# Last 256 columns' residual added in PSUM, last stores in three pieces, first chunk's last k tile by tile, and longer side distances in a one-core decoder trunk

## The chip, the cores and the metric

The kernel runs on one core of a Trainium2 chip. It has five engines with a queue each: TensorE (PE, matrix products and transposes), VectorE (DVE), ScalarE (ACT), GpSimd (POOL) and SyncE (SP, which here issues DMA transfers). Time is in device microseconds, the median of several executions. A profile of one execution gives the start and length of each instruction; "span" is the time from the first to the last event of the core in it.

## The reference

One layer of a decoder: RMSNorm, one input projection whose columns feed three groups (a gated short convolution, a convolution over 31 taps with layer norm, a cross-attention into 256 memory tokens), an output projection, the residual, a final RMSNorm. It is done for a prompt of 1024 tokens and for 8 samples of 8 tokens, which have states and caches of their own.

```python
h = rmsnorm(x, g_norm); proj = h @ w_in
...
out_a = bg_a * conv_a * jax.nn.silu(z_a)
out_b = jax.nn.silu(layernorm(conv_b, ln_g, ln_b)) * jax.nn.silu(z_b)
out_x = cross_attn(q, mk, mv) * jax.nn.silu(z_x)
mixed = jnp.concatenate([out_a, out_b, out_x], axis=-1)
return x + mixed @ w_out, new_ctx_a, new_ctx_b
...
y_prompt = rmsnorm(yp, g_final)
y_sample = rmsnorm(ys, g_final)
```

All is float32 (widths: model 1024, groups 384, 384 and 256).

## The kernel before

**Products in three passes.** PE multiplies values in the type `float32r`. To keep float32's precision, each operand is split into a high part (a cast, mostly on ACT) and a low part (the difference, on DVE), and a product is the sum of three: high by high, low by high, high by low. The normalized and transposed tokens are `hh` and `hl` (one pair of tiles for each k, a block of 128 of the 1024 model columns), the weights are `wh` and `wl`, the output weights `woh` and `wol`, the mixed activations `mh` and `ml`. `pass_k(n, c, ps, p, k)` is one such product: column tile n, chunk c of the tokens, pass p (0 is `hh` by `wh`, 1 is `hh` by `wl`, 2 is `hl` by `wh`), block k.

**Startup (`startup`, an order written out by hand).** The first four column tiles run over four chunks of tokens: 256, 256, 256 and 320 (`HEAD`). For the first chunk the four accumulators `acc` take up all four banks of the pool `mmp` (`MM()`); `p(k, j)` is pass j of block k for the four tiles. `x_tr` transposes a block of the raw tokens into a bank of a second pool of four (`sdp`, `SD()`), `x_ev_hi` makes `hh` of it on ACT, `x_ev_lo` makes `hl` on DVE; the bank is free after both. `n0` to `n3` are the norms of the chunks; `square` sums squares on ACT (tile `junk`, 128x1024), `r_bc` makes the factors and `r_tr` transposes them into a row `rrow`, by which DVE multiplies each accumulator of the first two chunks when it evacuates it (`evac`; the four evacuations write `u`, `u`, `u` and `sig`). The second chunk's accumulators take the same four banks, so each waits for one evacuation of the first. Weights of the first tiles are loaded in halves of 512 columns (`hw_load`), cast by `hw_hi` and subtracted by `hw_lo`.

**Side work.** After startup the order on each engine is made by a scheduler from the program's order. The projection of a tile (`proj`) calls `side()` after each four products; it takes one entry of the queue `steps`, work of another kind that PE does in between. `None` entries are distances: places at which nothing is done, so that the other engines have time for what the next entry needs. `S0` to `S3` are the distances in the sample attention: `sa_scores`, S0, `sa_norm` (DVE makes the probabilities `Ps`), S1, `sa_pT` (PE transposes `Ps`, DVE copies them to `Pts`), S2, `sa_pv` (PE multiplies `Pts` with the cached values, ACT copies to `Os`), S3, `sa_out`. Between, DVE runs the 31 taps of the second convolution (`accB`).

**Output.** `out_tile` computes a tile of 128 tokens by 1024 columns in two banks, adds the residual `xres` on DVE, sums squares on ACT, and scales and stores. The last tile is `out_last`: it goes in three parts of 512, 256 and 256 columns, and for each part DVE adds the residual out of PSUM (`xr`), ACT sums squares, and DVE multiplies with -0.5 and the final gain into `yg`. Behind the third part come root, reciprocal and one correction step (`y`, `v`, `y0`, `t`, `r`), and the scaling by r in two pieces, 576 columns on DVE and 448 on ACT, each stored by one transfer (SP and ACT issue them).

Of the kernel before, what the change touches and what calls it, by code (L numbers as in the profile page):

```python
# [10 lines left out]
F32R = mybir.dt.float32r  # L11
# [5 lines left out]
KT = 8  # L17
# [8 lines left out]
A0, A1, A2, A3, A4, A5 = 2, 9, 5, 3, 3, 1  # L26
S0, S1, S2, S3 = 4, 3, 4, 2
L0, L1, L2 = 1, 3, 2
# [13 lines left out]
def hybrid_trunk_kernel(  # L42
# [91 lines left out]
    warm = cst.tile([128, 1], F32, name="warm")  # L134
    ident = cst.tile([128, 128], F32, name="ident")
    graw = cst.tile([8, 128], F32, name="graw")
    gT = cst.tile([128, 16], F32, name="gT")
# [145 lines left out]
    def hw_hi(k, copy):  # L283
        if k % 2 == 0:
            hwh[k // 2] = B("wh", F32R, D)
            hwl[k // 2] = B("wl", F32R, D)
        copy(hwh[k // 2][:, hsl(k)], hrw[k // 2][:, hsl(k)])  # L287

# [638 lines left out]
    def out_tile(i, hook=None):  # L927
# [4 lines left out]
        for n, k in enumerate(worder):  # L932
            if hook:
                hook(n)
            for f in range(2):
                cs = slice(f * 512, f * 512 + 512)
                if sample:
                    st = ms[0][:, k * 128:k * 128 + 128]
                    mm(banks[f], st, wo_h[k][:, cs], n == 0, False, 216)
                    mm(banks[f], st, wo_l[k][:, cs], False, n == KT - 1, 216)  # L940
                else:
                    out_mm(banks[f], i, n, k, cs)
        ss = SM("oss", 2)
# [17 lines left out]

    def out_mm(bank, i, n, k, cs):
        w = cs.stop - cs.start
        a, b = mh[k][:, i * 128:i * 128 + 128], ml[k][:, i * 128:i * 128 + 128]
        mm(bank[:, :w], a, wo_h[k][:, cs], n == 0, False, w / 2.4)
        mm(bank[:, :w], b, wo_h[k][:, cs], False, False, w / 2.4)
        mm(bank[:, :w], a, wo_l[k][:, cs], False, n == KT - 1, w / 2.4)

    def out_last(i):
# [3 lines left out]
        pre = SM("opre", 1)  # L973
        parts = [slice(0, 512), slice(512, 768), slice(768, 1024)]
        for f, cs in enumerate(parts):
            w = cs.stop - cs.start
            bank = MM()
            for n, k in enumerate(worder):
                out_mm(bank, i, n, k, cs)
            V.tensor_tensor(xr[:, cs], bank[:, :w], xr[:, cs], ALU.add)  # L980
            junk = SD()
            S.activation(junk[:, :w], xr[:, cs], AF.Square, accum_out=ss[:, f:f + 1])
            if f == 1:
                V.tensor_tensor(pre, ss[:, 0:1], ss[:, 1:2], ALU.add)
                V.tensor_scalar(pre, pre, 1.0 / D, EPS, ALU.mult, ALU.add)
            V.scalar_tensor_tensor(yg[:, cs], xr[:, cs], -0.5, gf[0][:, cs], ALU.mult, ALU.mult)

# [5 lines left out]
        V.scalar_tensor_tensor(r, t, -3.0, y0, ALU.add, ALU.mult)  # L993
        a, b = slice(0, 576), slice(576, 1024)
        dst = y_prompt[0, i * 128:i * 128 + 128]
        V.tensor_scalar(yg[:, a], yg[:, a], r, None, ALU.mult)
        S.activation(yg[:, b], yg[:, b], AF.Copy, scale=r)  # L997
        nc.sync.dma_start(dst[:, a], yg[:, a])
        nc.scalar.dma_start(dst[:, b], yg[:, b])

# [6 lines left out]
    def startup():  # L1007
# [142 lines left out]
        S.copy(rrow[0][:, RAW:RAW + 256], rps[:, :256])  # L1150
        n1.square(0)
        t1 += [x_tr(1, 2), x_tr(1, 3)]
        p(7, 0)
        x_ev(1, 2, t1[2])
        x_ev(1, 3, t1[3])
        n1.square(1)
        for n in range(NHEAD):
            for j in (2, 1):
                pass_k(n, 0, acc[n], j, KT - 1, 1)
            evac(n, 0, acc[n])  # L1160
        acc = [MM() for _ in range(NHEAD)]
        for k in range(KT):
# [4 lines left out]
            if k + 4 < KT:  # L1167
                t1.append(x_tr(1, k + 4))
            if k == 3:
                r_bc(n1, 256)  # L1170
        n2.square(0)
# [184 lines left out]
```

## Time and profile before

| | |
|---|---|
| three runs | 473.11, 472.13, 474.51 us; median 473.11 |
| the profiled execution | 472.01 us, span 470.2 us |
| DVE, ACT busy | 333.4 us (71%), 229.5 us (49%) |
| HBM read and written | 34.81 MB, 5.42 MB (86 GB/s over the span) |

Times of instructions are counted from the span's start. A line of the timeline has the start, the length, the engine and line, the operation with its output and inputs (buffer numbers left out), shapes, and the count of merged instructions; in square brackets stands how long the engine stood idle before it, and who ended that. `L59` is the helper through which all of VectorE's instructions go and `L95` and `L102` are those of products and transposes, so that one has to go by the names of tiles. The view of waits has, for each pair of a waiting and a waited-for group, the sum, the number and the longest.

### The profile page before, as it was taken

To read this page: it belongs to the slowest core of one execution; us is meant where nothing else is said; L and a number is where in the kernel's file an instruction comes from. 1 tells how busy PE (TensorE), PEld (TensorE's weight loads), DVE (VectorE), ACT (ScalarE), POOL (GpSimd) and SP (SyncE) were. 2 spreads that over 40 slices of the span, in tenths; PEclk is the share of its full clock that TensorE was granted. 3 is DMA by queue.
4 is the path that set the end of the run, shared out by engine and by line. 5 is a ranking of instruction groups with operands and counts; after the bars stand their busy time and mean duration, and the time that the engine had idled before them with its cause. 6 is when DMAs were issued, how large, how long until landed. Compare 5 with 4: busy or idle time off the path is not lost.

```text
span 470.2 us, 7495 instructions
## 1 busy us (share of the span) xinstructions
PE 459.7 (98%) x2931; PEld 435.1 (93%) x2931; DVE 333.4 (71%) x593; ACT 229.5 (49%) x584; POOL 4.2 (1%) x20
## 2 busy tenths in 40 slices
PE   8999999999999999999999989999999999999994
PEld 8899999999999999999999879999999888888884
DVE  4769999999878999996899965237353537333333
ACT  5785659600223648565795364595542534111112
POOL 2000000000000000000000000000000000000000
PEclk9999999999999999999999999999999999999998
DMA  8931253100460300422021102113401634311111
GB/s 295 370 93 46 71 153 91 45 1 0 128 187 16 119 1 1 135 57 80 12 79 46 43 3 62 45 46 105 164 2 45 233 147 129 118 45 46 45 67 68
DMA packets 36447, 40.44 MB, mean 86 GB/s; under 512 B 1743, under 2 KB 30453, under 8 KB 36405
## 3 DMA queue, kind: packets, MB, share of 16 engines
q1 hardware_dynamic: 35965, 39.21, 25.7%
q10 hardware_dynamic: 448, 0.76, 0.5%
q8 instruction: 23, 0.38, 0.3%
q14 instruction: 11, 0.09, 0.1%
HBM read 34.81 MB, written 5.42 MB: 86 GB/s over the span
## 4 chain that ended last, share of the span: by engine, by line
PE 86%; DVE 11%; DMA 1%; issue 1%; ACT 1%; ACTq 0%; DVEq 0%
PE mm L95 76%; DVE accB L59 6%; PE sd L95 5%; PE sd L102 4%; DVE tA L59 1%; DVE wl L59 1%; DMA wr<-in_w_in_dram 1%; DVE red L59 1%; PE sd L874 1%; DVE mx L59 0%; DVE s L59 0%; ACT junk L187 0%; DVE hl L59 0%; ACT yg L997 0%; ACTq L1011 0%
## 5 line engine op out<-in xcount | busy, mean ns | idle before, releaser
L95 PE MATMUL mm<-hh,wh 128*128 128x384 f32 (+2 forms) x632 | 118.9, 324 | 1.1 <-DVE u L59 0.8
L95 PE MATMUL mm<-hl,wh 128*128 128x384 f32 (+2 forms) x632 | 118.6, 323 | 0.0
L59 DVE SCALAR_TENSOR_TENSOR accB<-u,prm,accB 128x1024 f32<-128x1024 f32 x90 | 115.4, 1282 | 1.5
L95 PE MATMUL mm<-hh,wl 128*128 128x384 f32 (+2 forms) x632 | 116.4, 321 | 0.0
L95 PEld LDWEIGHTS mm<-hh,wh 128*128 128x128 f32 x632 | 101.9, 188 | 2.8 <-DVE u L59 1.0
L95 PEld LDWEIGHTS mm<-hl,wh 128*128 128x128 f32 x632 | 101.7, 188 | 0.7 <-issue 0.6
L95 PEld LDWEIGHTS mm<-hh,wl 128*128 128x128 f32 x632 | 101.6, 188 | 0.4
L95 PE MATMUL mm<-woh,ml 128*128 128x512 f32 (+1 forms) x136 | 51.2, 377 | 0.0
L95 PE MATMUL mm<-wol,mh 128*128 128x512 f32 (+1 forms) x136 | 51.2, 377 | 0.0
L95 PE MATMUL mm<-woh,mh 128*128 128x512 f32 (+1 forms) x136 | 51.2, 377 | 0.0
L59 DVE TENSOR_TENSOR xres<-mm,xres 128x512 f32<-128x512 f32 (+2 forms) x19 | 12.4, 662 | 39.7 <-PE mm L95 39.5
L952 ACT ACTIVATE sd<-xres 128x512 f32<-128x512 f32 (+1 forms) x16 | 9.6, 600 | 57.9 <-DVE xres L59 57.9
L59 DVE TENSOR_TENSOR wl<-wr,wh 128x512 fp32r<-128x512 f32 x50 | 33.4, 688 | 4.2 <-ACT wh L287 2.2
L95 PEld LDWEIGHTS mm<-woh,mh 128*128 128x128 f32 x136 | 25.6, 188 | 4.7
L95 PEld LDWEIGHTS mm<-woh,ml 128*128 128x128 f32 x136 | 25.6, 188 | 4.7
L95 PEld LDWEIGHTS mm<-wol,mh 128*128 128x128 f32 x136 | 25.6, 188 | 4.6
L310 ACT CAST wh<-wr 128x512 fp32r<-128x512 f32 x42 | 24.4, 620 | 1.7 <-issue 1.3
L362 ACT ACTIVATE prod<-us,prm 128x64 f32<-128x64 f32 x93 | 24.9, 345 | 0.1
L510 ACT ACTIVATE sz<-mm 128x384 f32<-128x384 f32 (+1 forms) x24 | 11.4, 474 | 23.3 <-PE mm L95 23.1
L712 ACT ACTIVATE P<-sd,nb 128x256 f32<-128x256 f32 x32 | 14.7, 473 | 13.2 <-DVE nb L59 12.3
L433 ACT ACTIVATE sig<-mm 128x384 f32<-128x384 f32 (+1 forms) x6 | 2.8, 474 | 37.4 <-PE mm L95 37.3
L249 ACT ACTIVATE hh<-sd,gT 128x256 fp32r<-128x256 f32 (+1 forms) x32 | 14.3, 491 | 7.1 <-PE sd L102 6.8
(198 smaller groups left out, 527.9 us busy)
## 6 DMA issues: line engine op xcount, KB each, us to landing
wr<-in_w_in_dram SPq DMA_DIRECT2D x21, 512.0 KB
wor<-in_w_out_dram SPq DMA_DIRECT2D x8, 512.0 KB
xres<-in_x_prompt_dram SPq DMA_DIRECT2D x8, 512.0 KB
out_dram<-xres SPq DMA_DIRECT2D x7, 512.0 KB
x<-in_x_prompt_dram SPq DMA_DIRECT2D x6, 512.0 KB
cache<-in_cache_mem_k_dram SPq DMA_DIRECT2D x8, 256.0 KB
cache<-in_cache_mem_v_dram SPq DMA_DIRECT2D x8, 256.0 KB
wr<-in_w_in_dram SPq DMA_DIRECT2D x6, 256.0 KB
```

The costliest lines, as they stand in the source:

```text
L59: r = f(*a, **k)
L95: T.matmul(out, lhsT, rhs, start=start, stop=stop)
L102: T.transpose(out, in_, ident[:n, :n])
L249: S.activation(hh[k][:, off:off + n], ps[:, :n], AF.Copy, scale=gT[:, k:k + 1])
L310: S.copy(dst_hi[:, a:b], src[:, a:b])
L362: S.activation(p3[:, k, :], src, AF.Copy, scale=w[:, k0 + k:k0 + k + 1])
L433: S.activation(sig[j][:, off:off + n], ps[:, :n], AF.Sigmoid)
L510: S.activation(sz[0][:, off:off + n], ps[:, :n], AF.Silu)
L712: S.activation(P_[i][:, h * 256:h * 256 + 256], bank[h // 2][:, (h % 2) * 256:(h % 2) * 256 + 256], AF.Exp, bias=nb[:, h:h + 1], scale=SCA ...
L874: T.transpose(ps[:, j * 128:j * 128 + 128], accB[j][:, lncols[i]:lncols[i] + 128], ident)
L952: S.activation(junk[:rows], xr[:rows, cs], AF.Square, accum_out=ss[:rows, f:f + 1])
```

## The change

It has four parts.

1. `S1` goes from 3 to 7 and `S2` from 4 to 6: `sa_pT` stands four places later behind `sa_norm`, and `sa_pv` six places later than before.
2. In startup the last block (k = 7) of the first chunk is no longer multiplied pass by pass over the four tiles, but tile by tile with all three passes, each tile's evacuation right behind. The transposes of the next chunk's block 3 stand behind the first tile; the low parts `hl` of the blocks 2 and 3 of the next chunk stand behind the four evacuations. The squares of the second norm and its factors move later.
3. The first weight cast (`hw_hi(0)`) goes in two instructions of 256 columns instead of one of 512.
4. In `out_last` the residual of the last 256 columns is split into `rh` and `rl`, and PE adds both to the bank with a product by a unit matrix (`identr`, the cast of `ident`). DVE's addition falls away, and the square and the multiplication read the bank. The last scaling goes in three pieces: 320 and 320 columns on DVE, 384 on ACT, each with its own store.

```diff
-S0, S1, S2, S3 = 4, 3, 4, 2
+S0, S1, S2, S3 = 4, 7, 6, 2
...
-        copy(hwh[k // 2][:, hsl(k)], hrw[k // 2][:, hsl(k)])
+        c0 = (k % 2) * 512
+        for a in (range(c0, c0 + 512, 256) if k == 0 else ()):
+            copy(hwh[0][:, a:a + 256], hrw[0][:, a:a + 256])
+        if k:
+            copy(hwh[k // 2][:, hsl(k)], hrw[k // 2][:, hsl(k)])
...
+        rh, rl = B("rh", F32R, 256), B("rl", F32R, 256)
+        S.copy(identr, ident)
+        split(rh, rl, xr[:, parts[2]], 0, 256)
         for f, cs in enumerate(parts):
             w = cs.stop - cs.start
             bank = MM()
+            if f == 2:
+                mm(bank[:, :w], identr, rh, True, False, w / 2.4)
+                mm(bank[:, :w], identr, rl, False, False, w / 2.4)
             for n, k in enumerate(worder):
-                out_mm(bank, i, n, k, cs)
-            V.tensor_tensor(xr[:, cs], bank[:, :w], xr[:, cs], ALU.add)
+                out_mm(bank, i, n + (f == 2), k, cs, n == KT - 1)
+            res = bank[:, :w] if f == 2 else xr[:, cs]
+            if f < 2:
+                V.tensor_tensor(res, bank[:, :w], res, ALU.add)
             junk = SD()
-            S.activation(junk[:, :w], xr[:, cs], AF.Square, accum_out=ss[:, f:f + 1])
+            S.activation(junk[:, :w], res, AF.Square, accum_out=ss[:, f:f + 1])
...
-            V.scalar_tensor_tensor(yg[:, cs], xr[:, cs], -0.5, gf[0][:, cs], ALU.mult, ALU.mult)
+            V.scalar_tensor_tensor(yg[:, cs], res, -0.5, gf[0][:, cs], ALU.mult, ALU.mult)
...
-        a, b = slice(0, 576), slice(576, 1024)
-        V.tensor_scalar(yg[:, a], yg[:, a], r, None, ALU.mult)
-        S.activation(yg[:, b], yg[:, b], AF.Copy, scale=r)
-        nc.sync.dma_start(dst[:, a], yg[:, a])
-        nc.scalar.dma_start(dst[:, b], yg[:, b])
+        for cs in (slice(0, 320), slice(320, 640)):
+            V.tensor_scalar(yg[:, cs], yg[:, cs], r, None, ALU.mult)
+            nc.sync.dma_start(dst[:, cs], yg[:, cs])
+        cs = slice(640, 1024)
+        S.activation(yg[:, cs], yg[:, cs], AF.Copy, scale=r)
+        nc.scalar.dma_start(dst[:, cs], yg[:, cs])
...
-        n1.square(0)
-        t1 += [x_tr(1, 2), x_tr(1, 3)]
-        p(7, 0)
-        x_ev(1, 2, t1[2])
-        x_ev(1, 3, t1[3])
-        n1.square(1)
+        t1.append(x_tr(1, 2))
+        x_ev_hi(1, 2, t1[2])
         for n in range(NHEAD):
-            for j in (2, 1):
+            for j in (0, 2, 1):
                 pass_k(n, 0, acc[n], j, KT - 1, 1)
+            if n == 0:
+                t1.append(x_tr(1, 3))
+                x_ev_hi(1, 3, t1[3])
+                n1.square(0)
             evac(n, 0, acc[n])
+        x_ev_lo(1, 2, t1[2])
+        x_ev_lo(1, 3, t1[3])
...
-            if k == 3:
-                r_bc(n1, 256)
+            if k == 4:
+                n1.square(1)
+        r_bc(n1, 256)
```

**The head on DVE.** This is DVE's queue from the two oldest low parts of the second chunk (blocks 0 and 1) on, before the change. `sd` is a bank with transposed tokens, `mm` an accumulator of the first chunk.

```order
L59 SCALAR_TENSOR_TENSOR hl_125<-sd_343,gT,hh_124 128x256
L59 SCALAR_TENSOR_TENSOR hl_127<-sd_346,gT,hh_126 128x256
L59 SCALAR_TENSOR_TENSOR hl_129<-sd_371,gT,hh_128 128x256
L59 SCALAR_TENSOR_TENSOR hl_131<-sd_374,gT,hh_130 128x256
L59 TENSOR_TENSOR u_389<-mm_168,rrow_155 128x256
L59 TENSOR_TENSOR u_394<-mm_169,rrow_155 128x256
L59 TENSOR_TENSOR u_399<-mm_170,rrow_155 128x256
L59 TENSOR_TENSOR sig_404<-mm_171,rrow_155 128x256
```

And this is the same place in the change (all buffer numbers are shifted):

```order
L59 SCALAR_TENSOR_TENSOR hl_126<-sd_345,gT,hh_125 128x256
L59 SCALAR_TENSOR_TENSOR hl_128<-sd_348,gT,hh_127 128x256
L59 TENSOR_TENSOR u_384<-mm_169,rrow_156 128x256
L59 TENSOR_TENSOR u_390<-mm_170,rrow_156 128x256
L59 TENSOR_TENSOR u_396<-mm_171,rrow_156 128x256
L59 TENSOR_TENSOR sig_402<-mm_172,rrow_156 128x256
L59 SCALAR_TENSOR_TENSOR hl_130<-sd_371,gT,hh_129 128x256
L59 SCALAR_TENSOR_TENSOR hl_132<-sd_378,gT,hh_131 128x256
```

The four evacuations have moved ahead of the low parts of blocks 2 and 3.

**The head on PE.** In the change PE's queue has at that place, from the transposes of block 2 on, the following rows; `mm_169` and `mm_170` are the accumulators of tiles 0 and 1. (Before, the transposes of both blocks came first, then four `hh` by `wh` products, one for each tile, then the other passes.)

```order
L102 MATMUL sd_371<-ident,x_110 128x128
L102 MATMUL sd_371<-ident,x_115 128x128
L95 MATMUL mm_169<-hh_139,wh_311 128x256
L95 MATMUL mm_169<-hl_140,wh_311 128x256
L95 MATMUL mm_169<-hh_139,wl_312 128x256
L102 MATMUL sd_378<-ident,x_110 128x128
L102 MATMUL sd_378<-ident,x_115 128x128
L95 MATMUL mm_170<-hh_139,wh_311 128x256
L95 MATMUL mm_170<-hl_140,wh_311 128x256
L95 MATMUL mm_170<-hh_139,wl_312 128x256
```

Tile 0 is complete after three products, while the transposes of block 3 have moved behind it. On ACT the square of the second chunk's second token tile now stands between the `hh` of block 4 and of block 5; before, both squares stood ahead of block 4.

**The sample attention on PE.** Before, the transposes of `Ps` stand in the last pass of a chunk of 320 columns:

```order
L95 MATMUL mm_3120<-hl_131,wh_2860 128x320
L102 MATMUL sd_3144<-ident,Ps_3079 128x128 x2
L95 MATMUL mm_3120<-hl_133,wh_2860 128x320
L95 MATMUL mm_3120<-hl_135,wh_2860 128x320
L95 MATMUL mm_3120<-hl_137,wh_2860 128x320
L95 MATMUL mm_3120<-hl_139,wh_2860 128x320
L102 MATMUL sd_3153<-ident,Ps_3086 128x128 x2
```

In the change they stand in the second pass of the next chunk, of 384 columns:

```order
L95 MATMUL mm_3158<-hh_131,wl_3053 128x384
L102 MATMUL sd_3171<-ident,Ps_3081 128x128 x2
L95 MATMUL mm_3158<-hh_133,wl_3053 128x384
L95 MATMUL mm_3158<-hh_135,wl_3053 128x384
L95 MATMUL mm_3158<-hh_137,wl_3053 128x384
L95 MATMUL mm_3158<-hh_139,wl_3053 128x384
L102 MATMUL sd_3180<-ident,Ps_3088 128x128 x2
```

They have moved behind sixteen products. On DVE the two copies to `Pts` have moved behind the two evacuations `tA<-sz` of 384 and 320 columns and the low parts that follow these.

**The end on DVE.** The square brackets name the engines whose semaphores an instruction waits for. Before:

```order
L59 TENSOR_TENSOR xres_4579<-mm_4794,xres_4579 128x256 [waits PE_49]
L59 SCALAR_TENSOR_TENSOR yg_4731<-xres_4579,gf_3769 128x256 [waits DVE_49]
L59 SCALAR_TENSOR_TENSOR v_4824<-oss_4732,opre_4733 128x1 [waits Activation_49]
L59 RECIPROCAL y_694_4825<-y_4823 128x1 [waits Activation_49]
L59 SCALAR_TENSOR_TENSOR t_4826<-y_694_4825,v_4824 128x1 [waits DVE_49]
L59 SCALAR_TENSOR_TENSOR t_696_4827<-t_4826,y_694_4825 128x1 [waits DVE_49]
L59 TENSOR_SCALAR yg_4731<-yg_4731,t_696_4827 128x576 [waits DVE_49]
```

In the change:

```order
L59 SCALAR_TENSOR_TENSOR yg_4733<-mm_4801,gf_3771 128x256 [waits Activation_49]
L59 SCALAR_TENSOR_TENSOR v_4832<-oss_4734,opre_4735 128x1 [waits DVE_49]
L59 RECIPROCAL y_696_4833<-y_4831 128x1 [waits Activation_49]
L59 SCALAR_TENSOR_TENSOR t_4834<-y_696_4833,v_4832 128x1 [waits DVE_49]
L59 SCALAR_TENSOR_TENSOR t_698_4835<-t_4834,y_696_4833 128x1 [waits DVE_49]
L59 TENSOR_SCALAR yg_4733<-yg_4733,t_698_4835 128x320 [waits DVE_49]
L59 TENSOR_SCALAR yg_4733<-yg_4733,t_698_4835 128x320
```

The addition is gone, the multiplication reads the bank `mm` and waits for ACT (for its square of the same bank) instead of DVE, and the last scaling is two rows. On PE two products, `mm_4801<-rh_4736,identr` and `mm_4801<-rl_4737,identr`, stand ahead of the last 24.

More of the change, by code (lines that the diff above doesn't have):

```diff
@@ L135, in hybrid_trunk_kernel @@
     ident = cst.tile([128, 128], F32, name="ident")
+    identr = cst.tile([128, 128], F32R, name="identr")
     graw = cst.tile([8, 128], F32, name="graw")
@@ L941, in out_tile @@
                 else:
-                    out_mm(banks[f], i, n, k, cs)
+                    out_mm(banks[f], i, n, k, cs, n == KT - 1)
         ss = SM("oss", 2)
@@ L960, in out_tile, with out_mm @@
         nc.sync.dma_start(dst, xr[:rows])
-    def out_mm(bank, i, n, k, cs):
+    def out_mm(bank, i, n, k, cs, last):
         w = cs.stop - cs.start
@@ L966, in out_mm @@
         mm(bank[:, :w], b, wo_h[k][:, cs], False, False, w / 2.4)
-        mm(bank[:, :w], a, wo_l[k][:, cs], False, n == KT - 1, w / 2.4)
+        mm(bank[:, :w], a, wo_l[k][:, cs], False, last, w / 2.4)
     def out_last(i):
```

## The prediction

> **What bounds the kernel now.** I read the page first, then what TensorE (PE) waits for, then three places in the timeline.
>
> ```profile
> span 470.2 us, 7495 instructions
> PE 459.7 (98%) x2931; PEld 435.1 (93%) x2931; DVE 333.4 (71%) x593; ACT 229.5 (49%) x584; POOL 4.2 (1%) x20
> ...
> PE 86%; DVE 11%; DMA 1%; issue 1%; ACT 1%; ACTq 0%; DVEq 0%
> ```
>
> PE is busy for 459.7 of 470.2 us and carries 86% of the chain that ended last. So little can be won except where PE stands still, or before its first and behind its last matmul. Its waits, in the view of waits filtered to PE, leaving out the launch's own (1.4 us, not touched) and one of 0.2:
>
> ```profile
> PE sd L102 <- DVE Ps L59: 1.3, 1, 1.3
> PE mm L95 <- DVE u L59: 0.8, 1, 0.8
> PE mm L95 <- DVE wh L59: 0.3, 1, 0.3
> ```
>
> These three are what the edits of the side distances, of the head and of the start aim at. The tail is what DVE, ACT and the stores do after PE's end. I take the four places in the order of the program.
>
> **Start: the first weight cast in two halves.**
>
> ```profile
> 5.78 0.84 ACT L249 ACTIVATE hh<-sd,gT 128x256 fp32r<-128x256 f32 x2 [2.05 <-PE sd L102]
> ...
> 5.94 0.43 DVE L59 CAST wh<-wr 128x512 fp32r<-128x512 f32 x1 [0.37 <-DMA wr<-in_w_in_dram]
> ...
> 6.51 0.72 PE L95 MATMUL mm<-hh,wh 128*128 128x256 f32 x4 [0.34 <-DVE wh L59]
> ```
>
> The first product waits for the whole cast, which ends at 6.37. Half of it would be there at about 6.15; the other operand, the first of two hh at 5.78 + 0.84/2, near 6.25. The start 0.14 after the later one gives about 6.38, so **0.13 us** are won, between 0 (a later weight DMA decides) and 0.2. The second cast costs DVE a few hundredths, hidden by the 0.3 us until its next result is due. The new cast of the identity stands on ACT before the first hh, in ACT's 2.05 us of idleness there; without that cover it would cost about 0.3 (the row of 18.62 below shows 0.37 for a 128x256 ACT copy).
>
> **Head: the last k of the first chunk, tile by tile.**
>
> ```profile
> 18.62 0.37 ACT L1150 COPY rrow<-sd 128x256 f32<-128x256 f32 x1 [1.07 <-PE sd L102]
> 18.72 0.87 DVE L59 SCALAR_TENSOR_TENSOR hl<-sd,gT,hh 128x256 fp32r<-128x256 f32 x2
> 18.89 1.06 ACT L187 ACTIVATE junk<-x 128x1024 f32<-128x1024 f32 x1
> 19.05 0.44 PE L102 MATMUL sd<-ident,x 128*128 128x128 f32 x2 [0.24 <-ACT rrow L1150]
> ...
> 19.80 0.28 PE L95 MATMUL mm<-hl,wh 128*128 128x256 f32 x1
> 19.92 0.28 PE L95 MATMUL mm<-hh,wl 128*128 128x256 f32 x1
> ...
> 20.45 0.88 DVE L59 SCALAR_TENSOR_TENSOR hl<-sd,gT,hh 128x256 fp32r<-128x256 f32 x2 [0.85 <-ACT hh L249]
> ...
> 21.24 1.08 DVE L59 TENSOR_TENSOR u<-mm,rrow 128x256 f32<-128x256 f32 x3
> ...
> 21.71 1.38 PE L95 MATMUL mm<-hh,wh 128*128 128x256 f32 x4 [0.80 <-DVE u L59]
> ...
> 22.23 0.42 DVE L59 TENSOR_TENSOR sig<-mm,rrow 128x256 f32<-128x256 f32 x1
> ...
> 22.93 0.38 PE L102 MATMUL sd<-ident,x 128*128 128x128 f32 x2
> ...
> 23.34 0.47 ACT L249 ACTIVATE hh<-sd,gT 128x256 fp32r<-128x256 f32 x1 [1.21 <-PE sd L102]
> ...
> 23.62 0.38 PE L102 MATMUL sd<-ident,x 128*128 128x128 f32 x2
> ```
>
> Read it from 21.71 backwards. The second chunk's four products each need a bank that one of DVE's four evacuations (u, u, u, sig) frees. These start at 21.24 because two hl stand ahead of them in DVE's queue; the hl wait for hh, and hh for ACT's square of 1.06 us (junk). The four products then take 1.22 us instead of four times 0.12 (the step from 19.80 to 19.92).
>
> In the change the evacuations stand ahead of those two hl, and a tile's three products stand together. PE: the transposes of block 2 keep their place, tile 0's three products run from about 18.65 to 19.15, the next transposes still start at 19.05 to 19.1 (they wait for rrow, 18.62 + 0.37), and nine products at 0.12 from 19.25 issue by 20.3. DVE: the two older hl are through at 18.72 + 0.87 = 19.59; from then on one evacuation each 0.33 (from 21.24 to 22.23 are three steps), so sig starts at 20.55 instead of 22.23. The next transposes stood 0.70 behind sig (22.93); now at 21.25. That is **1.68 us** earlier.
>
> What is late next? ACT now has a square between hh of k = 4 and of k = 5. With x_tr at 21.25 and one k each 0.69 (transposes and four products, 22.93 to 23.62), PE wants k = 5 at 23.9; ACT begins hh of k = 4 at 21.66 (0.41 behind the transposes, as 23.34 behind 22.93), the square at 22.05, hh of k = 5 at 23.1 and is done by 23.6. The cover is 0.3; if it is gone, up to 0.5 is lost. Later hh follow at 0.4 on ACT against 0.48 on PE. The two hl that went behind the evacuations free their banks by 21.75, due at 22.6 and 23.3. Some rescaling moves forward on DVE between 30 and 41, the number of instructions there stays. I count 1.68 within 1.2 to 1.8.
>
> Does it last to the end? DVE is busy almost throughout from 60 to 275, so PE could run into it later. These rows speak against that:
>
> ```profile
> DVE u L59 <- ACT sig L433: 3.6, 4, 1.2
> ...
> 224.29 1.29 DVE L59 TENSOR_REDUCE mx<-sd 128x2 f32<-128x512 f32 x2 [3.02 <-PE sd L95]
> ```
>
> The first is from DVE's waits between 60 and 276, the second the place where the long DVE stretch of the chain begins: there DVE itself stood 3.02 us idle for PE. An earlier PE therefore takes DVE with it.
>
> **Sample attention: side distances S1 from 3 to 7, S2 from 4 to 6.**
>
> ```profile
> 269.76 1.55 PE L95 MATMUL mm<-hl,wh 128*128 128x384 f32 x8
> 271.14 1.33 PE L95 MATMUL mm<-hh,wh 128*128 128x320 f32 x8
> 272.31 1.34 PE L95 MATMUL mm<-hh,wl 128*128 128x320 f32 x8
> 273.48 0.75 PE L95 MATMUL mm<-hl,wh 128*128 128x320 f32 x4
> 275.57 0.41 PE L102 MATMUL sd<-ident,Ps 128*128 128x128 f32 x2 [1.34 <-DVE Ps L59]
> ```
>
> PE stands 1.34 us for Ps, with products queued behind that need nothing of it. Four more side places are 16 products, 4 of 320 and 12 of 384 columns; at 0.146 (272.31 to 273.48, eight) and 0.173 (269.76 to 271.14, eight) that is 2.66 us of work, which covers 1.34 with 1.3 to spare. So **1.34 us** go. If DVE did not follow the head's 1.8, the need would be 3.15 and 0.5 would be waited. Behind it: the two Pts copies now stand behind two evacuations on DVE, and the products that read Pts come 28 products later (4.8 us against a copy of 0.42); the output of the samples moves by six places and is still ahead of the layer norm's first transposes, whose order is unchanged. Nothing else is late.
>
> **Tail.**
>
> ```profile
> 463.58 0.28 PE L95 MATMUL mm<-wol,mh 128*128 128x256 f32 x1
> 463.90 0.42 DVE L59 TENSOR_TENSOR xres<-mm,xres 128x256 f32<-128x256 f32 x1 [1.46 <-PE mm L95]
> 464.36 0.42 DVE L59 SCALAR_TENSOR_TENSOR yg<-xres,gf 128x256 f32<-128x256 f32 x1
> 464.42 0.39 ACT L982 ACTIVATE sd<-xres 128x256 f32<-128x256 f32 x1 [2.36 <-DVE xres L59]
> ...
> 464.96 0.16 DVE L59 SCALAR_TENSOR_TENSOR v<-oss,opre 128x1 f32<-128x1 f32 x1 [0.18 <-ACT sd L982]
> ...
> 465.29 0.16 DVE L59 RECIPROCAL y<-y 128x1 f32<-128x1 f32 x1 [0.17 <-ACT y L989]
> ...
> 465.93 0.52 DVE L59 TENSOR_SCALAR yg<-yg,t 128x576 f32<-128x576 f32 x1
> ...
> 466.63 0.35 ACTq L999 DMA_DIRECT2D out_dram<-yg  x1
> ...
> 122.15 0.76 DVE L59 COPY kd<-sd 128x256 f32<-128x256 f32 x2 [0.39 <-ACT kv L664]
> ```
>
> The addition between PE's end and ACT's square goes: 464.42 - 463.90 = -0.52. Two products of 256 columns are added on PE: +0.24. The split of the residual (a cast on ACT, a subtraction on DVE) stands five output tiles earlier in the order, where both engines mostly wait for PE, and is hidden; uncovered it would be about 0.8. DVE's multiplication yg stood beside the square; now it waits for it (the order shows it) and stands ahead of v and the reciprocal. It holds DVE for 0.33 to 0.40 (the steps of u and of hl in the head), and v takes a short step more, so that the reciprocal comes, by my estimate, 0.46 behind the square's sum instead of 0.33 (464.96 to 465.29): +0.13. A wait of this kind is in the trace: at 122.15 DVE's copy of a bank waited for ACT's copy out of it, though neither reads what the other writes. The Trainium skill has the reason, in "PSUM — Partial Sum Buffer", section "PSUM bank collisions raise a hardware error": two engines must not touch one bank at once, reads included. By that rule the term is +0.13, without it 0; the trace agrees with the rule.
>
> The stores: DVE's first piece of 320 columns is ready about 0.2 sooner than 576 were, so the first transfer starts 0.2 sooner; the last issue stays near 466.65, since an issue takes 0.35 and SP has two, and ACT's piece shrinks by 64 columns of 448. I take -0.1, between -0.2 and +0.5 (three transfers of smaller rows in place of two; no row has such sizes). Tail: -0.52 + 0.24 + 0.13 - 0.1 = **-0.25**, between -0.4 and +0.35.
>
> **Sum.** 0.13 + 1.68 + 1.34 + 0.25 = 3.4 us off the span of 470.2: 466.8. The profiled execution took 472.01, 1.8 more than its span, and would become 468.6. It lies 1.1 under the median of the three runs (473.11) and at their lowest (472.13); runs scatter upwards by some 2 us, so I name 469.0 for the median.
>
> **The rivals.**
> 1. DVE takes part of the head back (0.17). If its backlog keeps its place in time, PE gains the 1.34, of the head only what the longer distance covers, and the stall on ACT's square costs 0.5: 3.4 - 0.5 - 0.5 to 3.4 - 1.8, that is 1.6 to 2.4 off, 470 to 471. For it: DVE's busy share there; against it: its idle 3.02 us at 224.
> 2. The change doesn't do what it says (0.07): the banks are freed no sooner since the wait only moves from u to another releaser, such as hh of k = 5, and the stores eat the tail. Then the 1.34 is most of it: within 1.5 of before, 471.5 to 472.5.
> 3. Slower (0.04): the granted clock. With fewer pauses the mean 0.996 might fall; 459.7 us of PE times 0.01 are 4.6 us. Below 0.988 all is given back, below 0.983 the kernel is 0.5% slower, 476. Against it stands, below the mean of the whole span, the row of the stretch from 94 to 130, whose columns end with clock, DMA share and GB/s:
>
> ```profile
> core 0: 470.2 us, clock 0.996
> ...
> 94.00:130.00 36.00, 36.00 (x206) 34.43 (x205) 34.35 (x46) 3.63 (x7) 0.00 (x0) 1.00 0.16 45
> ```
>
> PE works there without a pause and is granted 1.00. For it is only that the runs shown differ by 2.4 us, which nothing in the profile explains.
>
> **How the numbers follow.** The forecast has 0.72, with 467.3 to 470 as its own range. With rivals 1 and 2 the range is 466.8 to 471.8; the rest is the slower case and ends beyond. A measurement here tells about 0.5% from no change, 2.4 us. Faster by more: the forecast, 0.72. Within: rivals 1, which lies about on that line, and 2: 0.24. Slower: 0.04.
>
> **What would show it.** In the new profile: first product near 6.4; sig at 20.4 to 20.6, and transposes at 21.1 to 21.3 with no wait for u over 0.3; no wait for Ps; the square within 0.1 of PE's end, yg behind it, three stores. Wrong would be: a PE wait on hh near 24, on Ps near 273, or any new one over 0.5 between 60 and 290; an end of the span over 3.8 us behind the last store's issue (466.63 to 470.2 now, 3.6).

## The result, and the profile after

| | before | after |
|---|---|---|
| median of 6 runs | 472.72 us (472.13 to 474.51) | 469.72 us (469.15 to 470.64) |
| profiled execution, its span | 472.01, 470.2 us | 469.15, 467.3 us |
| ratio, 95% interval | | 0.9935 (0.9917 to 0.9952) |

The kernel is 0.65% faster, 3.0 us by the medians and 2.9 by the spans; 3.4 off the span and 469.0 us were forecast. First the page of the changed kernel (span, busy time, the chain of work that ended last), then PE's waits:

```profile
span 467.3 us, 7506 instructions
PE 459.4 (98%) x2933; PEld 435.6 (93%) x2933; DVE 332.9 (71%) x595; ACT 229.2 (49%) x586; POOL 4.1 (1%) x20
...
PE 98%; DVE 0%; ACT 0%; issue 0%; POOL 0%; DVEq 0%; ACTq 0%; POOLq 0%
```

```profile
PE mm L1046 <- POOL ss L183: 1.4, 1, 1.4
PE mm L95 <- ACT hh L250: 0.5, 1, 0.5
```

PE's busy time is the same, though two products were added; only its pauses went. The waits for `Ps` and for `u` are gone. The chain had 11% of DVE, the stretch up to `Ps`; now it is PE from end to end. What is left beside the launch is a pause of 0.45 before the first product. The timeline at the start, in the head and at the place of `Ps`:

```profile
6.01 0.49 DVE L59 CAST wh<-wr 128x256 fp32r<-128x256 f32 x2 [0.61 <-DMA wr<-in_w_in_dram]
6.46 0.71 PE L95 MATMUL mm<-hh,wh 128*128 128x256 f32 x4 [0.45 <-ACT hh L250]
7.69 0.62 ACT L292 CAST wh<-wr 128x512 fp32r<-128x512 f32 x1 [1.25 <-DMA wr<-in_w_in_dram]
8.37 0.75 PE L95 MATMUL mm<-hh,wh 128*128 128x256 f32 x4
...
18.39 0.42 PE L102 MATMUL sd<-ident,rrow 128*128 128x128 f32 x2
19.73 1.16 DVE L59 TENSOR_TENSOR u<-mm,rrow 128x256 f32<-128x256 f32 x3
20.62 1.07 PE L95 MATMUL mm<-hh,wh 128*128 128x256 f32 x4
20.82 0.42 DVE L59 TENSOR_TENSOR sig<-mm,rrow 128x256 f32<-128x256 f32 x1
21.53 0.38 PE L102 MATMUL sd<-ident,x 128*128 128x128 f32 x2
...
274.68 0.86 PE L95 MATMUL mm<-hh,wl 128*128 128x384 f32 x4
275.38 0.38 PE L102 MATMUL sd<-ident,Ps 128*128 128x128 f32 x2
```

`sig` starts at 20.82 instead of 22.23, the next transposes at 21.53 instead of 22.93. But the transposes of `rrow`, which stood at 18.16, come at 18.39: the start has lost 0.23. ACT's cast of the second block's weights waited until 7.69 for its transfer (7.29 before), and PE's first product of that block began at 8.37 instead of 8.23, which is 0.14 of the 0.23. From the transposes of `rrow` on, the head takes 3.14 us instead of 4.77. The tail:

```profile
461.02 0.28 PE L95 MATMUL mm<-wol,mh 128*128 128x256 f32 x1
461.39 0.37 ACT L996 ACTIVATE sd<-mm 128x256 f32<-128x256 f32 x1 [2.15 <-PE mm L95]
461.67 0.19 ACT L996 ACTIVATION_READ_ACCUMULATOR sd<-mm 128x1 f32 x1
461.90 0.29 ACT L1003 ACTIVATE y<-oss,opre 128x1 f32<-128x1 f32 x1
461.90 0.42 DVE L59 SCALAR_TENSOR_TENSOR yg<-mm,gf 128x256 f32<-128x256 f32 x1 [2.27 <-ACT sd L996]
462.24 0.15 DVE L59 SCALAR_TENSOR_TENSOR v<-oss,opre 128x1 f32<-128x1 f32 x1
462.31 0.15 DVE L59 RECIPROCAL y<-y 128x1 f32<-128x1 f32 x1
...
462.94 0.68 DVE L59 TENSOR_SCALAR yg<-yg,t 128x320 f32<-128x320 f32 x2
...
463.59 0.36 ACTq L1014 DMA_DIRECT2D out_dram<-yg  x1
```

The square follows the last product's start by 0.37 instead of 0.84 (464.42 - 463.58). DVE's `yg` waits for ACT's read-out of the same bank, as the order said. From the square to the reciprocal it takes 0.92 instead of 0.87, from the first scaling to the end of the span 4.36 instead of 4.27.

### The profile page after: what moved, and what is told of

It is laid out like the page before. It is cut to its first block, busy times and chain, and to the rows that moved or that the text cites. A ratio compares the mean times of both kernels' runs of the same rounds, so it can differ in the third digit from the quotient of the medians.

```text
span 467.3 us, 7506 instructions
## 1 busy us (share of the span) xinstructions
PE 459.4 (98%) x2933; PEld 435.6 (93%) x2933; DVE 332.9 (71%) x595; ACT 229.2 (49%) x586; POOL 4.1 (1%) x20
## 4 chain that ended last, share of the span: by engine, by line
PE 98%; DVE 0%; ACT 0%; issue 0%; POOL 0%; DVEq 0%; ACTq 0%; POOLq 0%
PE mm L95 85%; PE sd L95 6%; PE sd L102 6%; PE mm L1046 1%; PE sd L879 1%; ACT hh L250 0%; DVE yg L59 0%; DVE t L59 0%; PE sd L853 0%; PE sd L848 0%; DVEq L1370 0%; POOL ident masks.py:199 0%; ACT sd L996 0%; PE sd L230 0%; PE mm L1072 0%
## 5 line engine op out<-in xcount | busy, mean ns | idle before, releaser
L59 DVE TENSOR_TENSOR accB<-sz,accB 128x384 f32<-128x384 f32 (+1 forms) x9 | 4.8, 535 | 17.3 <-ACT sz L515 17.3
```

Of the source, the lines that this page charges most:

```text
L59: r = f(*a, **k)
```

## The experiments

The start scatters, so in each profile I count from the transposes of `rrow`. The columns: start of DVE's first weight cast (the landing of these weights, where DVE waits for nothing else); start of the transposes of `rrow`; from there to the transposes of the next chunk's block 4 (the head); from there to the start of PE's last product; from that to the end of the span (the tail); span behind the transposes of `rrow`.

| profile | cast | rrow | head | to PE's last | tail | span behind rrow |
|---|---|---|---|---|---|---|
| before | 5.94 | 18.16 | 4.77 | 445.42 | 6.62 | 452.0 |
| after | 6.01 | 18.39 | 3.14 | 442.63 | 6.28 | 448.9 |
| e1_dist_only | 6.04 | 18.44 | 4.75 | 443.97 | 6.69 | 450.7 |
| e2_head_only | 7.16 | 19.38 | 3.14 | 443.87 | 6.65 | 450.5 |
| e3_s1_4 | 5.97 | 18.31 | 3.14 | 443.68 | 6.31 | 450.0 |
| e4_evac_first | 6.01 | 18.40 | 3.83 | 443.32 | 6.28 | 449.6 |
| e5_low_first | 7.18 | 20.78 | 3.96 | 443.47 | 6.25 | 449.7 |
| e6_one_cast | 6.15 | 19.10 | 3.12 | 442.61 | 6.29 | 448.9 |
| e7_two_stores | 6.03 | 18.96 | 3.13 | 442.60 | 6.24 | 448.8 |
| e8_dve_add | 6.92 | 19.01 | 3.14 | 442.37 | 6.72 | 449.1 |
| e9_head2 | 6.89 | 18.98 | 3.14 | 442.44 | 6.28 | 448.7 |
| e10_start | 5.04 | 18.90 | 3.15 | 442.63 | 6.17 | 448.8 |
| e11_best | 5.06 | 18.85 | 3.14 | 442.39 | 6.16 | 448.6 |
| e12_idle | 7.63 | 19.66 | 3.13 | 442.64 | 6.30 | 448.9 |

**The distances alone** (5 rounds of runs).

```diff
 # kernel before
-S0, S1, S2, S3 = 4, 3, 4, 2
+S0, S1, S2, S3 = 4, 7, 6, 2
```

> The kernel before with S1 = 7 and S2 = 6 and nothing else. Theory (the wait for Ps is PE's alone and more products cover it): no wait of PE for Ps, nothing new over 0.3 us behind it, span 470.2 - 1.34 = 468.9, some 1.3 us under the kernel before. Rival (the wait only moves, to Pts or to the output of the samples): a new wait of about 1 us between 275 and 300, span within 0.4 of 470.2.

Measured: 470.92 us against 472.48, ratio 0.9968 (0.9955 to 0.998). PE's waits in this kernel:

```profile
PE mm L1031 <- POOL ss L182: 1.4, 1, 1.4
PE mm L95 <- DVE u L59: 0.8, 1, 0.8
PE sd L102 <- DMA x<-in_x_prompt_dram: 0.4, 1, 0.4
PE sd L102 <- ACT rrow L1150: 0.2, 1, 0.2
```

No `Ps`, nothing new behind it; the one for `x` belongs to this execution's start. Behind `rrow` PE ends 445.42 - 443.97 = 1.45 sooner. The theory holds; its size is 0.1 too small.

**The head alone** (5 rounds of runs): the change's order of the last k (part 2), nothing else.

```diff
 # kernel before
-        n1.square(0)
-        t1 += [x_tr(1, 2), x_tr(1, 3)]
-        p(7, 0)
...
+        t1.append(x_tr(1, 2))
+        x_ev_hi(1, 2, t1[2])
         for n in range(NHEAD):
-            for j in (2, 1):
+            for j in (0, 2, 1):
                 pass_k(n, 0, acc[n], j, KT - 1, 1)
...
             evac(n, 0, acc[n])
+        x_ev_lo(1, 2, t1[2])
+        x_ev_lo(1, 3, t1[3])
...
```

> The kernel before with the new order of the first chunk's last k and nothing else. Theory (DVE follows an earlier PE, since at its long stretch it waits 3.0 us for PE): from the transposes of rrow to the next chunk's transposes of block 4 it takes 3.1 us instead of 4.8, PE's wait for Ps stays at 1.3, DVE's wait for PE at mx stays at 3.0, span 470.2 - 1.6 = 468.6. Rival (DVE's backlog keeps its place in time): the wait for Ps grows to about 2.9, or PE waits anew for DVE somewhere between 30 and 224, DVE's wait at mx shrinks by as much, and the span stays within 0.5 of 470.2.

Measured: 471.09 us, ratio 0.9967 (0.9956 to 0.9978). Here are PE's wait for `Ps`, and from DVE's waits between 60 and 290 the one at `mx`:

```profile
PE sd L102 <- DVE Ps L59: 1.3, 1, 1.3
```

```profile
DVE mx L59 <- PE sd L95: 5.1, 2, 3.0
```

Had DVE kept its place, PE would now wait some 2.9 for `Ps`, and DVE's 3.0 at `mx` would have shrunk. Neither moved: an earlier PE takes DVE along, and the gain of the head (4.77 - 3.14 = 1.63; 1.55 of it left at PE's end) lasts. This execution's span, 469.9, shows only 0.3 of it, since its first weights landed 1.2 us later (7.16); the medians show 1.4 of it (472.48 - 471.09). The two parts add: 0.32% and 0.33% against 0.65% of the change.

**One place instead of four** (one run).

```diff
 # changed kernel
-S0, S1, S2, S3 = 4, 7, 6, 2
+S0, S1, S2, S3 = 4, 4, 4, 2
```

> The changed kernel with S1 = 4 and S2 = 4. Theory (cover is the products between, 4 of 320 columns for one place, 0.146 us each): one place covers 0.58 of the 1.34, a wait for Ps of 0.76 is left, span 467.3 + 0.76 = 468.1. Rivals: the longer S2 did it, or the place does not count by products: 1.34 are left, span 468.6; or one place was enough: no wait, 467.3.

```profile
272.74 0.60 PE L95 MATMUL mm<-hl,wh 128*128 128x320 f32 x3
274.08 0.41 PE L102 MATMUL sd<-ident,Ps 128*128 128x128 f32 x2 [0.74 <-DVE Ps L59]
```

0.74 were left of 1.34; 0.76 were expected. So a distance covers what its products take. The cost is larger than the row says: PE ends 443.68 - 442.63 = 1.05 later than in the changed kernel. About half of the difference is in how the pause is counted: three products from 272.74 on, 0.146 each, would let the next instruction start at 273.18, 0.90 before 274.08, while the 0.74 are counted from the last one's modelled end. In the same way the pause of the kernel before, 1.34 by its row, is 1.51 between issue steps (four products from 273.48 on end their steps at 274.06, and the transposes start at 275.57); taking it away was worth 1.45 (above). The last 0.15 (S2 has changed too) I have not told apart.

**DVE's order without PE's and ACT's** (one run).

```diff
 # changed kernel, in the head
+        n1.square(0)
+        t1 += [x_tr(1, 2), x_tr(1, 3)]
+        p(7, 0)
+        x_ev_hi(1, 2, t1[2])
+        x_ev_hi(1, 3, t1[3])
+        n1.square(1)
-        t1.append(x_tr(1, 2))
-        x_ev_hi(1, 2, t1[2])
         for n in range(NHEAD):
-            for j in (0, 2, 1):
+            for j in (2, 1):
                 pass_k(n, 0, acc[n], j, KT - 1, 1)
-            if n == 0:
-                t1.append(x_tr(1, 3))
-                x_ev_hi(1, 3, t1[3])
-                n1.square(0)
             evac(n, 0, acc[n])
         x_ev_lo(1, 2, t1[2])
         x_ev_lo(1, 3, t1[3])
...
```

> The changed kernel with PE's and ACT's old order in the head (pass by pass, both squares ahead of block 4), but DVE's new one: the four evacuations ahead of the low parts of blocks 2 and 3. Counted from the transposes of rrow, sig started at 4.07 before and at 2.43 after, the transposes of block 4 at 4.77 and 3.14. Theory (DVE's order brings the larger part, the tile-by-tile products the rest): tile 0 is complete at 2.04, three evacuations of 0.33 bring sig to 3.1, the transposes to 3.8: 0.65 us behind the changed kernel. Rivals: DVE's order does all (sig at 2.4), or it does nothing without the tiles (sig at 4.0).

```profile
18.40 0.42 PE L102 MATMUL sd<-ident,rrow 128*128 128x128 f32 x2
...
20.53 1.09 DVE L59 TENSOR_TENSOR u<-mm,rrow 128x256 f32<-128x256 f32 x3 [0.72 <-PE mm L95]
21.54 0.41 DVE L59 TENSOR_TENSOR sig<-mm,rrow 128x256 f32<-128x256 f32 x1
...
22.23 0.38 PE L102 MATMUL sd<-ident,x 128*128 128x128 f32 x2
```

`sig` 3.14 and the transposes 3.83 behind `rrow`; 3.1 and 3.8 were expected. DVE now waits 0.72 for PE's first complete tile.

**PE's and ACT's order without DVE's** (one run).

```diff
 # changed kernel, in the head
-        x_ev_hi(1, 2, t1[2])
+        x_ev(1, 2, t1[2])
...
-                x_ev_hi(1, 3, t1[3])
+                x_ev(1, 3, t1[3])
...
-        x_ev_lo(1, 2, t1[2])
-        x_ev_lo(1, 3, t1[3])
```

> The changed kernel with PE's new order in the head (tile by tile), but the low parts of blocks 2 and 3 ahead of the evacuations on DVE, as before. Theory (the evacuations wait for hh of block 3 by way of its low part): hh of block 3 is done 1.84 us behind the transposes of rrow, its low part at 2.3, then four evacuations, sig at 3.3 and the transposes of block 4 at 4.0, 0.9 us behind the changed kernel. Rivals: the tiles alone bring it (transposes at 3.1), or nothing (4.8).

Measured: `sig` 3.27 and the transposes 3.96 behind `rrow`. So of the head's 1.63, either order alone brings 0.94 (4.77 - 3.83) or 0.81 (4.77 - 3.96), and both are needed for all of it. The 0.81 need not be the tiles': ACT's squares have moved behind the `hh` as well, and DVE's wait of 0.85 for `hh` (at 20.45 in the kernel before) is gone in this run; the two were not taken apart. The time of this run, 472.35, is 2.6 above the changed kernel though: see the last section.

**The start, the stores, the addition** (one run each): each takes one part of the change back.

```diff
 # changed kernel; e6: the first cast
-        for a in (range(c0, c0 + 512, 256) if k == 0 else ()):
-            copy(hwh[0][:, a:a + 256], hrw[0][:, a:a + 256])
-        if k:
-            copy(hwh[k // 2][:, hsl(k)], hrw[k // 2][:, hsl(k)])
+        copy(hwh[k // 2][:, hsl(k)], hrw[k // 2][:, hsl(k)])
 # e7: the stores
-        for cs in (slice(0, 320), slice(320, 640)):
...
+        a, b = slice(0, 576), slice(576, 1024)
...
 # e8: the residual
...
-                mm(bank[:, :w], identr, rh, True, False, w / 2.4)
-                mm(bank[:, :w], identr, rl, False, False, w / 2.4)
...
-            if f < 2:
-                V.tensor_tensor(res, bank[:, :w], res, ALU.add)
+            V.tensor_tensor(res, bank[:, :w], res, ALU.add)
```

> The changed kernel with the first weight cast in one instruction of 512 columns. Theory (the start of the second block is set by when its weights land, and that scatters from one execution to the next by 0.4 us): the first product starts at 6.4 to 6.6, the second block's first products anywhere between 8.2 and 8.4, so that the span lies within 0.3 of 467.3 on either side. Rival (the halves cost DVE time, which delayed the second block in the changed kernel by 0.14 to 0.23): ACT's cast of block 1 at 7.7 as in the changed kernel, but the second block's products at 8.2.

> The changed kernel with the last scaling and stores in two pieces, 576 and 448 columns, as before. Theory (the transfer's fixed time and its bytes count, not the number of pieces): from the first scaling to the end of the span 4.27 us as before against 4.36 with three pieces, within 0.15 of each other. Rival (three pieces bring 0.2 by an earlier first transfer, hidden by scatter): 4.5 or more.

> The changed kernel with the last 256 columns' residual added by VectorE, as before, and no unit-matrix products; the three stores stay. Theory: PE ends 0.24 sooner, the square starts 0.84 behind the last product's start instead of 0.37, the reciprocal comes 0.87 behind the square's start instead of 0.92; in sum from the last product's start to the end of the span 0.42 longer, 0.18 us slower in all, which only the rows can show. Rival (bank sharing with ACT's square gives back all): the same length, 0.24 faster.

With one cast, behind `rrow` the same to 0.1 us, and a start in which all three numbers of the expectation were missed (first product at 6.72, second block at 9.07, span 468.0): the landing scatters by more than the 0.4 us that it assumed. The second block's weights were late by more than in the changed kernel:

```profile
6.15 0.43 DVE L59 CAST wh<-wr 128x512 fp32r<-128x512 f32 x1 [0.57 <-DMA wr<-in_w_in_dram]
...
6.72 0.71 PE L95 MATMUL mm<-hh,wh 128*128 128x256 f32 x4
...
8.40 0.62 ACT L288 CAST wh<-wr 128x512 fp32r<-128x512 f32 x1 [1.48 <-DMA wr<-in_w_in_dram]
...
9.07 0.75 PE L95 MATMUL mm<-hh,wh 128*128 128x256 f32 x4 [0.47 <-ACT wh L288]
```

From the start of a whole cast to the first product it is 0.57 here and before (6.51 - 5.94). With halves it is 0.44 where the cast came last: in the profile with DVE's addition PE waited for `wh`, with the cast at 6.92 and the product at 7.36.

```profile
6.92 0.49 DVE L59 CAST wh<-wr 128x256 fp32r<-128x256 f32 x2 [1.60 <-DMA wr<-in_w_in_dram]
...
7.36 0.71 PE L95 MATMUL mm<-hh,wh 128*128 128x256 f32 x4 [1.44 <-DVE wh L59]
```

The halves are worth their 0.13 at that place. But the second block's products come no sooner than 0.67 behind ACT's cast of its weights (9.07 - 8.40; 8.37 - 7.69), which started anywhere between 7.3 and 8.4; there the 0.13 is mostly lost. The rival (the halves delay the second block) wanted its products at 8.2 with one cast; they came at 9.07, behind their transfer, and with ACT's cast at 8.40 its condition, a cast at 7.7, was not met. The run with the distances alone meets it: one whole cast, ACT's cast at 7.74, and the second block's products at 8.48, not 8.2. And the step from ACT's cast to the products is 0.67 with one cast as with halves, so the halves did not delay them.

Two stores instead of three: from the first scaling to the end of the span 4.32 (4.27, 4.34 and 4.30 in the kernel before and the two built on it; 4.23 to 4.38 in the ten profiles with three, the lowest two with the reordered loads below). The ranges overlap: neither a gain nor a loss by three pieces can be told.

With DVE's addition PE ends 442.63 - 442.37 = 0.26 sooner and the tail is 6.72 - 6.28 = 0.44 longer: 0.18 in sum, as expected. This is what the residual in PSUM is worth, by one execution of each kernel.

**Three versions that the profiles suggested** (5 rounds of runs each). The first covers what is left of the wait for the second chunk's banks:

```diff
 # changed kernel; e9
+        for k in (0, 1):
+            for n in range(NHEAD - 1):
+                pass_k(n, 1, acc[n], 0, k)
+        for k in (0, 1):
+            t1.append(x_tr(1, k + 4))
+            pass_k(NHEAD - 1, 1, acc[NHEAD - 1], 0, k)
-        for k in range(KT):
+        for k in range(2, KT):
```

> The changed kernel with one more change in the head: behind the first chunk's last products PE takes the next chunk's blocks 0 and 1 for the first three tiles, then the transposes of block 4, and only then the fourth tile, whose bank sig frees last. Theory (the 0.43 us that the next chunk's first four products take beyond their 0.48 are the wait for sig's bank, and work of other banks covers it): from the transposes of rrow to the products of the next chunk's block 2 it takes 0.4 to 0.5 us less than in the changed kernel (22.36 - 18.39 = 3.97 there), no wait for hh of block 5 over 0.2, and 0.4 us less from those transposes to the end of the span. Rival (ACT's squares and hh become the limit at once): a wait for hh between 22 and 25 and less than 0.15 us won.

Measured: 469.37 us, ratio 0.9935 (0.9922 to 0.9947). The products of block 2 start some 0.2 sooner behind `rrow`, and 0.2 are left at the end (442.63 - 442.44), half of what was expected: the group of six still takes 0.91 to the next transposes instead of six times 0.12, since the third tile's bank is not free yet either: its product starts 0.21 behind the second's (21.54 - 21.33).

```profile
21.21 1.07 PE L95 MATMUL mm<-hh,wh 128*128 128x256 f32 x6
22.12 0.38 PE L102 MATMUL sd<-ident,x 128*128 128x128 f32 x2
```

The second reorders the first loads, the third is both:

```diff
 # changed kernel; e10
-WARM = 8
+WARM = 7
...
-        x_half(0, 0, nc.sync)
+        hw_load(0, nc.scalar)
         nc.scalar.dma_start(graw, g_norm[0].rearrange("(k p) -> k p", p=128))
-        x_half(1, 0, nc.sync)
-        hw_load(0, nc.scalar)
+        for a in (0, 256):
+            for i in (0, 1):
+                x_part(i, a, a + 256, nc.sync)
         hw_load(1, nc.scalar)
...
         hw_load(2)
         for i in (0, 1):
-            x_half(i, 1, nc.sync)
+            x_part(i, 512, 1024, nc.sync)
```

> The changed kernel with another order of the first loads: the first tokens in columns 0 to 255, 256 to 511 and the rest instead of two halves, the first weights as ACT's first transfer, one warm-up product less, and the transposes of block 2 behind the first products. Theory (the start and its scatter are the landing of the first weights, behind 512 KB of tokens of which blocks 0 and 1 need half): the first product starts at 5.0 to 5.6 instead of 6.4 to 7.7, the transposes of rrow at 17.2 to 17.8 instead of 18.2 to 19.4, runs 0.8 to 1.4 us under the changed kernel and closer together. Rival (the transfers share the same engines and only the sum of bytes counts, or rows of 1 KB are slower): the second block's weights land as late as now (7.3 to 8.4), the transposes of rrow stay at 18.2 or later, no gain.

> Both of these together. Theory: the gains add, 1.2 to 1.8 us under the changed kernel, 468 us or less. Rival: with an earlier start the evacuations wait for rrow no less long, so that only the larger of the two is left.

Measured: 469.71 us, ratio 0.9943 (0.993 to 0.9956), and both together 469.56, 0.994 (0.9927 to 0.9952). 0.8 to 1.4 us under the changed kernel were expected of the reordered loads, 1.2 to 1.8 of both: neither came. The timeline of the reordered loads:

```profile
5.86 0.74 PE L95 MATMUL mm<-hh,wh 128*128 128x256 f32 x4 [0.35 <-ACT hh L250]
...
10.30 0.55 PE L102 MATMUL sd<-ident,x 128*128 128x128 f32 x3 [0.48 <-DMA x<-in_x_prompt_dram]
```

The first product starts 0.6 sooner, but at 10.30 PE waits for the rest of the tokens, and the transposes of `rrow` come at 18.90. The stretches show where it is lost (the last two columns are DMA share and GB/s): here, and then in the changed kernel,

```profile
7.00:8.00 1.00, 1.00 (x11) 1.00 0.72 227
8.00:9.00 1.00, 1.00 (x11) 1.00 0.94 242
```

```profile
7.00:8.00 1.00, 1.00 (x11) 1.00 1.06 408
8.00:9.00 1.00, 0.96 (x8) 1.00 1.06 406
```

Between 7 and 9 us the transfers run at 227 to 242 GB/s instead of 406 to 408, and what was gained by the order is lost again. The rows of 1 KB are not what is under way there: of the 259 packets between 7 and 9 us only 30 are under 2 KB (52 of 449 in the changed kernel). Most of the small ones moved between 3 and 6 us, at 290 to 375 GB/s, no slower than the changed kernel's transfers in these stretches (205 to 334). Whether the later issue of the next transfers does it stays open; with a share of 0.94 at 242 GB/s the packets also take longer than with 1.06 at 406. None of the three beats the changed kernel by what a measurement can tell.

**A pause at the start** (5 rounds of runs).

```diff
 # changed kernel
+        for _ in range(2):
+            V.memset(B("junk", cols=D), 0.0)
         hw_hi(0, V.tensor_copy)
```

> The changed kernel with two fills of 128x1024 on VectorE ahead of the first weight cast, so that PE stands still for some 1.5 to 2.2 us before its first product. In the profile of the run with the low parts first, PE stood 1.76 us there, and from 7.9 to 11.3 us the granted clock was 0.50; in those with 1.4 us or less it was 1.00. Theory (the length of the pause at the start decides the clock): at a pause over 1.7 us the clock is 0.50 for some 3.4 us behind the first product in most executions, their mean clock 0.994 or less instead of 0.996 to 0.998, and the time is longer by the pause's growth (1.1 to 1.7) and by 1.7 to 1.9 for the clock, 472.6 to 473.4. Rival (that was a single event of that execution, or depends on when the pause falls): clocks as in the changed kernel in most executions, and 470.8 to 471.6.

The profiled execution's pause was only 1.17 us, shorter than meant, since PE's transposes ahead of it ended at 6.84 instead of 6.00. So the theory's case, a pause over 1.7, was not reached in the one profile that there is, and its clock behind the pause is 1.00. (The view of waits puts the 1.17 down to ACT's cast of the second block's weights, which ends at 7.94. But in the profile with DVE's addition the same product starts ahead of that cast, at 7.36 against 7.60; what it needs is DVE's cast.) Measured: 470.41 us, ratio 0.9965 (0.9953 to 0.9978), below both ranges. Of six executions four have mean clocks of 0.998 to 0.999 and times of 470.36 to 470.43, two have 0.995 and 471.62 and 471.73. A clock that fell at the start in these two would fit, but it is not shown: they have no profile, and among the runs of the kernel before there is one with a mean of 0.995 that took 472.36 us, less than most of the others (472.23 to 473.06). Whether the length of the pause decides stays open. And a second thing: where the first product waits for DVE's cast (7.63, behind the fills) and no longer for a transfer, these four agree to 0.07 us, while the changed kernel's six lie 1.5 apart.

## Why the prediction was right, step by step

- **Start**: 0.13 forecast, 0.23 lost in the profiled execution, outside the term's own range of 0 to 0.2. The step "the first product waits for the whole cast" was right and its 0.13 stands (0.57 against 0.44), and so was its condition for winning nothing, "a later weight DMA decides": it decided, at the second block. What the term left out is that this landing scatters by more than the term is worth (ACT's cast of the second block's weights between 7.29 and 8.40); over executions I take it to be near 0.
- **Head**: 1.68 forecast, 1.63 measured in the head, 1.55 of it at PE's end. `sig` came 2.43 behind `rrow`'s transposes as against 4.07, and no wait for hh of k = 5 appeared near 24: the cover of 0.3 on ACT held. Both halves of the argument were needed: without the tile-by-tile products DVE waits 0.72 for PE and 0.69 of the gain is lost, without the evacuations ahead of the low parts 0.82 (3.83 and 3.96 against 3.14).
- **Does it last**: yes. DVE's 3.0 us at `mx` stayed with the head alone and in the change, and the wait for `Ps` stayed 1.3 with the head alone. Rival 1 is out.
- **Distances**: 1.34 forecast, 1.45 measured alone, 1.4 in the change (from block 4's transposes to PE's last product 440.65 before and 439.49 after, and 0.24 of it are the two added products). The term was undersized by 0.1, by how a pause on PE is counted. The cover by 0.146 us for a product was right: 0.74 left with one place, 0.76 expected.
- **Tail**: -0.25 forecast, -0.10 measured: -0.47 for the addition (-0.52), +0.24 for the products (0.26 by the run without them), +0.05 for `yg` behind the square instead of +0.13 (it did wait, but the square out of PSUM is 0.04 shorter, 0.28 instead of 0.32 to its read-out), +0.09 for the stores instead of -0.1. The stores were mis-sized: the first transfer is issued 0.42 behind the first scaling instead of 0.55, and the end does not follow it; the 0.09 is within the scatter of this stretch (4.23 to 4.38).
- **Clock**: 0.998 in the mean after, 0.996 before; rival 3 did not come. Its price was wrong too: the prediction spread a fall of the mean over PE's 459.7 us of work, while in both profiles the clock is 1.00 up to PE's end and what the mean lacks is lost behind it, where PE has nothing to do (last section).

In sum +0.23 - 1.63 - 1.40 - 0.10 = -2.9 against -3.4. Of the 0.5 that is missing, 0.36 is the start and 0.15 the tail; head and distances together are right to 0.02. Rival 2 is out with the two waits gone.

## What to carry to other kernels

Where one engine is busy 98% of the time, list its few pauses and ask of each what stands ahead of the releaser in *its* queue; here two low parts that nobody needed yet kept four banks closed. A pause is covered by moving independent products into it, counted by their issue step, and to know whether such a gain lasts, look where the engine that would have to follow stands idle for the first one. When gains are a few tenths of a per cent, measure in the trace from an instruction behind the noisy start: kernels that should be equal then agreed to 0.1 us here, where their spans differed by up to 1.3. And before a mean clock is given a price, look in which stretch the clock falls.

## What the runs showed of the hardware

**The scatter between the profiles is mostly the landing of the first loads.** With one order of loads (and without the fills), DVE's first weight cast started between 5.94 and 7.18 and ACT's next one between 7.29 and 8.40. Behind the transposes of `rrow` the changed kernel and its three variants that should equal it (one cast, two stores, the pause) took 448.8 to 448.9 us, though these transposes came between 18.39 and 19.66. I had written of the 2.4 us between runs that nothing in the profile explains them; in these profiles the start does, by its loads and in one by the clock (below). The single timed runs have no profile of their own, so for them it is inferred from the run with the pause.

**The mean clock of a run says little here.** The runs have means of 0.994 to 0.999. In all fourteen profiles, taken in stretches of 3 us, the granted clock is 1.00 up to PE's end, with the one exception below, and it falls to 0.50 behind it. In the kernel before PE's last product ends at 463.86 (the columns in front of clock, DMA share and GB/s are the engines' busy times, PE's first):

```profile
464.00:467.00 3.00, 0.00 (x0) 0.00 (x0) 1.97 (x7) 1.47 (x4) 0.00 (x0) 0.85 0.00 0
467.00:470.20 3.20, 0.00 (x0) 0.00 (x0) 0.00 (x0) 0.00 (x0) 0.00 (x0) 0.50 0.44 164
```

In stretches of 0.2 us the fall comes 2.2 us behind PE's end here and 4.3 us in the changed kernel (465.58 - 461.30); over the fourteen profiles it comes 2.0 to 5.3 us behind. Half the clock from 466.09 to the end at 470.2 takes 0.004 off the mean, from 465.58 to 467.3 it takes 0.002: that is all of the 0.996 and the 0.998, and it costs no time.

**PE's clock can halve behind a short pause.** In the run with the low parts first, the first weights landed at 7.18; the first product, and then the clock in the stretches that follow (columns: PE busy, clock, DMA share, GB/s):

```profile
7.62 0.96 PE L95 MATMUL mm<-hh,wh 128*128 128x256 f32 x4 [1.76 <-DVE wh L59]
```

```profile
7.00:8.00 1.00, 0.38 (x3) 0.94 1.03 393
8.00:9.00 1.00, 1.00 (x6) 0.50 1.06 408
9.00:10.00 1.00, 1.00 (x7) 0.50 1.07 406
10.00:11.00 1.00, 1.00 (x7) 0.50 1.00 397
11.00:12.00 1.00, 1.00 (x9) 0.85 1.05 393
```

From 7.9 to 11.3, 3.4 us, PE ran at half its clock: six to seven products in a us instead of eleven. From the first product to the transposes of `rrow` it took 13.16 us, against 11.65 in three profiles whose first product also waited for late weights (e2_head_only, e8_dve_add and e9_head2). The half clock so cost some 1.5 us, by one execution. Of the 3.2 us by which this run's span is longer than the changed kernel's, 1.2 lie ahead of the first product, 1.2 from there to `rrow` (11.93 there) and 0.8 in the head. The pause was 1.76 us; pauses of 1.37 and 1.44 in two other profiles left the clock at 1.00. The Trainium skill, in "TensorE: Matmul & The Clock Gate", section "What's actually happening", has the clock fall to half after at least one idle window of about 3.4 us, and rise again after a busy window of as long, by windows that run freely. The 3.4 us of half clock agree with the trace. That the fall takes 3.4 us of idleness does not: 1.76 us were enough here, with the fall 2.0 us behind the start of the pause (5.86 to 7.9), and behind PE's end it came after as little as 2.0 us. That this delay varies from 2.0 to 5.3 us is what freely running windows could give; no run here tests it.
